# Gated DeltaNet layer: diagonal blocks stored apart in whole pieces, and VectorE's order beside the inversion written down

## The chip, the cores and the metric

The kernel runs on one core of a Trainium2 chip. The metric is the device time of one execution in microseconds, as the median of several runs. Engines are named by what they are: TensorE (PE) multiplies matrices, VectorE (DVE), ScalarE (ACT) and GpSimd (POOL) work on elements, SyncE (SP) only issues transfers. Each engine has its own queue of instructions, and ScalarE and POOL issue transfers from theirs too.

## What is computed

One layer of an encoder trunk: a sequence of 1024 tokens of width 1024, float32, with two mixers in parallel (grouped-query attention and a gated DeltaNet), and an expert-choice mixture behind them. The change lies in the DeltaNet. It has 8 heads of 64, works in chunks of 64 tokens in both directions, and needs for each chunk, head and direction the inverse of a unit triangular 64x64 matrix I + N. Beside it go the projections of the attention and the gates, and the modulation of the layer by a conditioning vector:

```
mod = silu(c) @ W_ada + b_ada -> (shift1, scale1, gate1, shift2, scale2, gate2)
h  = RMSNorm(x) * (1 + scale1) + shift1
one combined projection h @ W_in -> [attn q | attn k | attn v | dn q | dn k | dn v | dn z | dn beta(fwd,bwd) | dn decay(fwd,bwd) | branch gates]
A: GQA (8 q heads, 2 kv heads, dim 64), ...
B: gated DeltaNet (8 heads, dk=dv=64), ... forward and backward chunked scans with separate beta/decay parameters, summed, ...
merged = sigmoid(gA) * (A @ W_attn_up) + sigmoid(gB) * (B @ W_dn_up);  x += gate1 * (merged @ W_o)
```

## The kernel before

The part that matters runs from 100 to 410 us. First come the twelve projections of the DeltaNet (dn_group), bound by TensorE. Then eight tiles of 128 tokens (dn_tile, j = 0 to 7): for each tile and direction d VectorE makes masks (rr), TensorE sums them (L486), ScalarE takes an exponential (e, L488), VectorE multiplies (e, at, e, nn; L490 to L498). The tile nn holds two chunks of N for 8 heads; it is stored to n_d in device memory by two DMAs on SP's queue (L500). Beside tiles 0, 2 and 4 (QKV) a projection of the attention goes in (qkv_group).

A 64x64 matrix is inverted by its two diagonal 32x32 blocks and one product. dn_blocks reads the diagonal blocks back from n_d so that each of 128 partitions (16 chunks by 8 heads) holds the two blocks of one chunk and head (the tiles nb): four DMAs after tile 5, four after tile 7, issued by ScalarE, in pieces of 32 numbers, 128 bytes. dn_invert then works on VectorE alone: 31 steps q, in each a multiplication (L533) and a subtraction (L537) for either direction; it is a generator that gives way in 8 places (INV), so it has parts 0 to 7: steps 1 to 6, 7 to 10, 11 to 13, 14 to 16, 17 to 19, 20 to 22, 23 to 26, 27 to 31.

Between the parts stand eight "fills": projections of the attention (qkv_group 3 to 5) and gates (gate_group 0 to 4). Each is 48 matmuls (24 pairs, 8 depth blocks of 3 products: high part of the weights by high and low part of the activations, low part of the weights by the high part). proj_load loads 512 KB of weights on POOL's queue (wraw, L269), ScalarE casts the high part (wh, L272) and VectorE subtracts it (the low part wl, L273). wh and wl have two buffers each. proj_ahead loads the next group's weights early and notes them in self.ahead, which holds one entry:

```python
    def proj_ahead(self, col):
        self.ahead = col, self.proj_load(col)
    def proj(self, col, n=128):
        if self.ahead and self.ahead[0] == col:
            wh, wl = self.ahead[1]
            self.ahead = None
        else:
            wh, wl = self.proj_load(col, n)
```

The loop asks for the next group's weights, then runs a group, then a part of the inversion, then two steps of the modulation (mod(MODS[1])). A modulation step adds a row block of W_ada times the conditioning vector to macc (L903, L905); each eighth also closes a block: ScalarE casts the sum to a high part (L889), POOL subtracts for the low part (L890), TensorE adds over partitions (L892), SP loads the bias into y (L894), VectorE adds (L895), SP stores. These y tiles, and those that hold a fill's result until it is stored (L1121, L1163), share two buffers.

A scheduler orders the instructions of each engine by priorities and its own times, except inside a manual_schedule block, which keeps the program's order on the engines named: before, each of the 31 steps is one such block on VectorE, and the scheduler may place other work between them. After the inversion w_d is stored, and the scan follows; its first transposes are L606, and while it runs late_fill gives TensorE more projections (L1147).

Of the kernel before, what the change touches and what calls it, by code (L numbers as in the profile page):

```python
# [20 lines left out]
NT = 8  # L21
# [58 lines left out]
class K:  # L80
# [386 lines left out]
    def dn_tile(self, j):  # L467
# [13 lines left out]
        for d in range(2):  # L481
# [17 lines left out]
            for x in range(2):  # L499
                nc.sync.dma_start(self.n_d[d, 2 * j + x].rearrange("h s c -> s h c"),  # L500
                                  nn[64 * x:64 * x + 64].rearrange("p (h c) -> p h c", c=64))

    def dn_blocks(self, j0, j1):

        for d in range(2):
            src = self.n_d[d, 2 * j0:2 * j1].rearrange("n h (b s) c -> (n h) b s c", b=2)
            for b in range(2):
                self.nc.scalar.dma_start(self.nb[d][16 * j0:16 * j1, b], src[:, b, :, b * 32:b * 32 + 32])

    def dn_invert(self, pool, parts):  # L510
# [13 lines left out]
        for q in range(1, 32):  # L524
            sub = []
            with self.tc.manual_schedule(engines={mybir.EngineType.DVE}):
                for d, (nb, w, tmp) in enumerate(zip(nbs, ws, tmps)):
                    j = 32 - q if d == 0 else q - 1
                    rows = slice(0, j) if d == 0 else slice(j + 1, 32)
                    cols = slice(j, 32) if d == 0 else slice(0, j + 1)  # L530
                    shp = [128, 2, rows.stop - rows.start, cols.stop - cols.start]
                    t = tmp[:, :, rows, cols]
                    nc.vector.tensor_mul(t, nb[:, :, rows, j:j + 1].to_broadcast(shp),  # L533
                                         w[:, :, j:j + 1, cols].to_broadcast(shp))
                    sub.append((w[:, :, rows, cols], t))
                for t, u in sub:
                    nc.vector.tensor_sub(t, t, u)  # L537
            cost += q * (32 - q) + 60
            if cost >= total / parts:
                cost -= total / parts  # L540
                yield
# [31 lines left out]
    def scan_load(self, t):  # L573
# [6 lines left out]
        for d in range(2):  # L580
# [4 lines left out]
            nsrc = self.n_d[d, n].rearrange("h (b s) (e c) -> b s h e c", b=2, e=2)  # L585
# [3 lines left out]
            nc.sync.dma_start(nf[f], nsrc[d, :, :, 1 - d, :])  # L589
# [396 lines left out]
    def mixer(self):  # L986
        nc, i = self.nc, self.i
        with ExitStack() as stm:
# [10 lines left out]
            self.n_d = dnp.tile([2, 16, 8, 64, 64], F, name="n_d")  # L999
# [23 lines left out]
            def mod(n):  # L1023
                for _ in range(n):
                    next(mods, None)

            with ExitStack() as st2:
# [15 lines left out]
                for j in range(NT):  # L1043
                    if j in QKV:
                        self.qkv_group(QKV.index(j))
                    self.dn_tile(j)
                    if j == 5:
                        self.dn_blocks(0, 4)
                self.dn_blocks(4, NT)
            with ExitStack() as st2:  # L1050
                fills = [(self.qkv_group, C_Q, g) for g in range(3, 6)]
                fills += [(self.gate_group, C_G, g) for g in range(NGA)]
                iv = self.pool(st2, "invert", side="right")
                inv = self.dn_invert(iv, INV)
                for n, (f, c, g) in enumerate(fills):
                    if n + 1 < len(fills):
                        with self.tc.high_priority(offset=0):
                            self.proj_ahead(fills[n + 1][1] + fills[n + 1][2] * 128)
                    f(g)
                    next(inv, None)  # L1060
                    mod(MODS[1])
                for _ in inv:
                    pass
                mod(1000)
                self.lo = nc.vector
# [559 lines left out]
```

## Time and profile before

| | before |
|---|---|
| median of 3 runs | 1783.05 us (1782.53 to 1787.27) |
| profiled execution | 1782.9 us |
| its span in the profile | 1780.7 us |
| busy: TensorE, VectorE, ScalarE, POOL | 93%, 82%, 52%, 14% of the span |
| mean granted clock of TensorE | 0.965 of full speed |

The profile lists one execution: the span is what the engines' records cover, and 2.2 us of the execution lie around it. Busy time of one engine says nothing about what it waited for; that is read from the waits and the timelines, where each idle time is put down to the instruction or transfer whose end released the engine.

### The profile page before, as it was taken

The page shows a single profiled execution, that of the slowest core. Times are in us where ns is not written, and L with a number is a line of the kernel's source. Part 1 is how long each engine was busy: PE and PEld are TensorE (multiplying, and loading weights), DVE is VectorE, ACT ScalarE, POOL GpSimd, SP SyncE. Part 2 cuts the span into 40 slices and gives each one's busy share as a digit, 9 for nine tenths or more (in the row PEclk, how much of TensorE's full clock was granted, in tenths as well). Part 3 has the DMA queues.
Part 4 walks back from the last instruction along what each step waited for, and adds up shares of the span by engine and source line. Part 5 has one row for each costly group of instructions (what it writes and reads, how often), then busy time and mean ns, then how long its engine had stood idle before and what let it go on. Part 6 is the DMA issues. An engine that isn't in the chain of part 4 may idle for free. (4 is left out here: it accounts for less than half of the span.)

```text
span 1780.7 us, 28660 instructions
## 1 busy us (share of the span) xinstructions
PE 1663.8 (93%) x10363; PEld 1333.4 (75%) x10363; DVE 1453.2 (82%) x2523; ACT 924.4 (52%) x1372; POOL 256.7 (14%) x287
## 2 busy tenths in 40 slices
PE   6999998389999999999999999939999999999997
PEld 4777876377887778778887778827777777777776
DVE  6899895965777667679998366889999999999997
ACT  5654522113332422268884133327777777777775
POOL 0041512021111100021111212220000110010000
PEclk8999999699999999899999999969999999999999
DMA  9466389256667775431114454569999999999991
GB/s 272 124 178 178 108 214 212 71 174 166 192 188 180 206 224 134 137 124 34 34 35 160 159 204 155 191 238 309 387 387 383 370 384 385 382 373 379 387 335 24
DMA packets 283053, 390.81 MB, mean 219 GB/s; under 512 B 78299, under 2 KB 151695, under 8 KB 282655
## 3 DMA queue, kind: packets, MB, share of 16 engines
q1 hardware_dynamic: 247103, 328.15, 55.5%
q0 software_dynamic: 12960, 47.19, 9.7%
q10 hardware_dynamic: 22848, 13.63, 2.7%
q8 instruction: 82, 1.34, 0.3%
q14 instruction: 60, 0.49, 0.1%
HBM read 330.14 MB, written 58.77 MB: 218 GB/s over the span
## 5 line engine op out<-in xcount | busy, mean ns | idle before, releaser
L1514 DVE TENSOR_TENSOR ew<-er,ew 128x1024 fp32r<-128x1024 f32 x384 | 452.2, 1219 | 30.1 <-ACT ew L1513 30.1
L1513 ACT CAST ew<-er 128x1024 fp32r<-128x1024 f32 x384 | 391.1, 1049 | 138.2 <-PE pj L1567 103.0
L1567 PE MATMUL pj<-ew,xT 128*128 128x512 f32 x1536 | 368.0, 396 | 4.5 <-DVE ew L1514 4.5
L1567 PEld LDWEIGHTS pj<-ew,xT 128*128 128x128 f32 x1536 | 283.3, 188 | 76.4 <-DVE ew L1514 19.5
L1584 PE MATMUL tr<-ew,aT 128*128 128x512 f32 x768 | 191.3, 398 | 0.0
L1584 PEld LDWEIGHTS tr<-ew,aT 128*128 128x128 f32 x768 | 139.7, 188 | 30.5 <-DVE ew L1514 3.5
L279 PE MATMUL pj<-hTh,wl 128*128 128x512 f32 (+1 forms) x368 | 118.6, 401 | 26.4 <-DVE wl L273 26.4
L279 PE MATMUL pj<-hTh,wh 128*128 128x512 f32 (+1 forms) x368 | 118.5, 402 | 3.6 <-ACT hTh L252 1.8
L279 PE MATMUL pj<-hTl,wh 128*128 128x512 f32 (+1 forms) x368 | 118.6, 399 | 1.4 <-DVE hTl L255 1.4
L272 ACT CAST wh<-wraw 128x1024 fp32r<-128x1024 f32 (+1 forms) x45 | 46.7, 1037 | 137.3 <-PE pj L279 66.5
L279 PEld LDWEIGHTS pj<-hTh,wl 128*128 128x128 f32 (+1 forms) x368 | 69.3, 189 | 43.5 <-DVE wl L273 27.0
L1590 POOL DMA_INDIRECT out_dram<-xe,idxT x16 | 37.1, 2317 | 405.6 <-DVE tok L1488 351.1
L269 POOL DMA_DIRECT2D wraw<-in_w_in_dram x42 | 37.7, 898 | 369.4 <-DVE wl L273 278.7
L834 DVE TENSOR_REDUCE am<-pj 128x1 f32<-128x1024 f32 x64 | 77.8, 1217 | 12.4 <-PE pj L829 11.8
L1193 PE MATMUL pj<-hTh,uw 128*128 128x512 f32 x256 | 83.5, 404 | 1.0 <-DVE uth L1199 0.5
L279 PEld LDWEIGHTS pj<-hTh,wh 128*128 128x128 f32 (+1 forms) x368 | 68.6, 190 | 19.8 <-ACT hTh L252 1.9
L1147 PE MATMUL pj<-hTh,wh 128*128 128x512 f32 x240 | 82.7, 412 | 0.0
L1147 PE MATMUL pj<-hTh,wl 128*128 128x512 f32 x240 | 81.9, 410 | 0.0
L279 PEld LDWEIGHTS pj<-hTl,wh 128*128 128x128 f32 (+1 forms) x368 | 68.7, 188 | 17.6 <-DVE hTl L255 2.0
L1147 PE MATMUL pj<-hTl,wh 128*128 128x512 f32 x240 | 81.3, 409 | 0.0
L836 ACT ACTIVATE ap<-pj,am 128x1024 f32<-128x1024 f32 x64 | 71.9, 1123 | 13.9 <-DVE am L834 8.5
L829 PE MATMUL pj<-kT,qT 128*128 128x512 f32 x256 | 77.0, 412 | 1.5 <-ACT ap L836 1.5
(373 smaller groups left out, 3144.5 us busy)
## 6 DMA issues: line engine op xcount, KB each, us to landing
er<-in_w_gate_dram SPq DMA_DIRECT2D x128, 512.0 KB, 7.2
er<-in_w_up_dram SPq DMA_DIRECT2D x128, 512.0 KB
er<-in_w_down_dram SPq DMA_DIRECT2D x128, 512.0 KB, 10.0
wraw<-in_w_in_dram POOLq DMA_DIRECT2D x42, 512.0 KB, 5.8
mw<-in_w_ada_dram SPq DMA_DIRECT2D x64, 256.0 KB, 3.6
wt<-in_w_ada_dram SPq DMA_DIRECT2D x16, 512.0 KB, 8.6
gate_d<-y ACTq DMA_DIRECT2D x32, 256.0 KB, 3.3
kv<-kv_d SPq DMA_DIRECT2D x32, 256.0 KB, 3.6
```

The lines of the kernel that those rows point to most:

```text
L269: (queue or nc.gpsimd).dma_start(raw[:, :, :n], self.i["w_in"][0, :, col:col + n].rearrange("(k p) c -> p k c", p=128))
L272: nc.scalar.copy(wh[:, :, :n], raw[:, :, :n])
L279: self.nc.tensor.matmul(ps[q][:n], w[:, k, :n], x[k][:, q * 512:(q + 1) * 512], start=(k == 0 and w is wh and x is self.hTh), stop=(k == 7 ...
L829: nc.tensor.matmul(ps[:, kh], qT[:, i * 128:(i + 1) * 128], self.kT[a][:, s, kh * 512:(kh + 1) * 512], start=(s == 0), stop=(s == 1), skip ...
L834: nc.vector.reduce_max(m, ps, axis=AX.X, negate=True)
L836: nc.scalar.activation(p, ps, AF.Exp, bias=m, scale=1.0, accum_out=self.rv[:, h, half * 4 + i:half * 4 + i + 1])
L1147: nc.tensor.matmul(ps[q], a[:, k], x[k][:, q * 512:(q + 1) * 512], start=(k == 0 and a is wh and x is self.hTh), stop=(k == 7 and a is wl))
L1193: nc.tensor.matmul(ps, w[:, k], v[k][:, qs], start=(k == 0 and p == 0), stop=(k == 3 and p == 2))
L1513: nc.scalar.copy(hi, raw)
L1514: nc.vector.tensor_sub(lo, raw, hi.bitcast(F))
L1567: nc.tensor.matmul(pg[m], x[:, 2 * kp + k], wi[:, k], start=(kp == 0 and k == 0 and n == 0), stop=(kp == 3 and k == 1 and n == 2))
L1584: nc.tensor.matmul(py[q], x[:, k], wi[:, q], start=(k == 0 and n == 0), stop=(k == 7 and n == 2))
```

## The change

It does four things. N is stored in parts: the two diagonal blocks of each chunk go to a new tensor nb_d, laid out as the inversion reads it, by four DMAs on SP's queue; the one off-diagonal quarter that the scan needs goes to a smaller n_d by two DMAs on POOL's queue. dn_blocks reads whole pieces of 8 KB per partition, on SP's queue, after tiles 2, 4, 6 and 7. The manual order on VectorE reaches around the whole loop of fills, inversion parts and modulation, so all of VectorE's work there keeps the program's order. And the weights of the first fill are asked for after tile 4.

```diff
             for x in range(2):
-                nc.sync.dma_start(self.n_d[d, 2 * j + x].rearrange("h s c -> s h c"),
-                                  nn[64 * x:64 * x + 64].rearrange("p (h c) -> p h c", c=64))
+                n = 2 * j + x
+                rows = lambda b, e: nn[64 * x + 32 * b:64 * x + 32 * b + 32].rearrange(
+                    "p (h c) -> p h c", c=64)[:, :, 32 * e:32 * e + 32]
+                for b in range(2):
+                    nc.sync.dma_start(self.nb_d[d, 8 * n:8 * n + 8, b].rearrange("h s c -> s h c"), rows(b, b))
+                nc.gpsimd.dma_start(self.n_d[d, n].rearrange("h s c -> s h c"), rows(d, 1 - d))
...
         for d in range(2):
-            src = self.n_d[d, 2 * j0:2 * j1].rearrange("n h (b s) c -> (n h) b s c", b=2)
-            for b in range(2):
-                self.nc.scalar.dma_start(self.nb[d][16 * j0:16 * j1, b], src[:, b, :, b * 32:b * 32 + 32])
+            self.nc.sync.dma_start(self.nb[d][16 * j0:16 * j1].rearrange("p b s c -> p (b s c)"),
+                                   self.nb_d[d, 16 * j0:16 * j1].rearrange("n b s c -> n (b s c)"))
...
         for q in range(1, 32):
             sub = []
-            with self.tc.manual_schedule(engines={mybir.EngineType.DVE}):
...
-            nc.sync.dma_start(nf[f], nsrc[d, :, :, 1 - d, :])
+            nc.sync.dma_start(nf[f], self.n_d[d, n].rearrange("h s c -> s h c"))
...
-                    if j == 5:
-                        self.dn_blocks(0, 4)
-                self.dn_blocks(4, NT)
+                    if j == QKV[-1]:
+                        self.proj_ahead(C_Q + len(QKV) * 128)
+                    if j in (2, 4, 6):
+                        self.dn_blocks(j - 2, j)
+                self.dn_blocks(6, NT)
...
-                for n, (f, c, g) in enumerate(fills):
...
+                with self.tc.manual_schedule(engines={mybir.EngineType.DVE}):
+                    for n, (f, c, g) in enumerate(fills):
+                        if n + 1 < len(fills):
+                            with self.tc.high_priority(offset=0):
+                                self.proj_ahead(fills[n + 1][1] + fills[n + 1][2] * 128)
+                        f(g)
+                        next(inv, None)
+                        mod(MODS[1])
+                    for _ in inv:
+                        pass
+                    mod(1000)
```

On VectorE, where the inversion begins, the order before has two low parts ahead of the memsets and one more between the first two multiplications (wtmp, wb and nb are the inversion's tiles; 128x2x31 is step 1):

```order
L273 TENSOR_TENSOR wl_3099<-wraw_3096,wh_3098 128x1024
L273 TENSOR_TENSOR wl_3105<-wraw_3102,wh_3104 128x1024
L520 MEMSET wb0_2838 128x32 x2
L520 MEMSET wb1_2843 128x32 x2
L533 TENSOR_TENSOR wtmp0_2842<-nb0_707,wb0_2838 128x2x31
L905 TENSOR_SCALAR macc_712<-mw2_711,cs_182 128x512
L273 TENSOR_TENSOR wl_3191<-wraw_3188,wh_3190 128x1024
L533 TENSOR_TENSOR wtmp1_2847<-nb1_708,wb1_2843 128x2x31
```

Afterwards, at the end of part 0 and of part 1 (steps 6 and 10), VectorE's order reads:

```order
L539 TENSOR_TENSOR wb1_2916<-wb1_2916,wtmp1_2920 128x2x26x6
L906 TENSOR_SCALAR macc_713<-mw0_710,cs_183 128x512
L904 SCALAR_TENSOR_TENSOR macc_713<-mw1_711,cs_183,macc_713 128x512
L273 TENSOR_TENSOR wl_2952<-wraw_2949,wh_2951 128x1024
L273 TENSOR_TENSOR wl_2958<-wraw_2955,wh_2957 128x1024
L535 TENSOR_TENSOR wtmp0_2915<-nb0_708,wb0_2911 128x2x25x7
...
L539 TENSOR_TENSOR wb1_2916<-wb1_2916,wtmp1_2920 128x2x22x10
L896 TENSOR_TENSOR y_3039<-y_3039,tr_3032 1x512
L904 SCALAR_TENSOR_TENSOR macc_713<-mw2_712,cs_183,macc_713 128x512
L904 SCALAR_TENSOR_TENSOR macc_713<-mw0_710,cs_183,macc_713 128x512
L273 TENSOR_TENSOR wl_3050<-wraw_3047,wh_3049 128x1024
L273 TENSOR_TENSOR wl_3056<-wraw_3053,wh_3055 128x1024
```

No low part stands ahead of the inversion any more; two stand behind each part, and the modulation's addition (L896 of the change) has a fixed place behind part 1.

On TensorE, behind the last of the tiles' products (L478), the order of the change begins with a matmul that reads one of these low parts, wl_2958, and the modulation's two matmuls (L893) stand four matmuls into the next group:

```order
L478 MATMUL dn_2759<-kq3_720 64x64 x4
L279 MATMUL pj_2961<-hTh0_405,wl_2958 128x512 x2
L279 MATMUL pj_2961<-hTh1_446,wh_2957 128x512 x2
...
L279 MATMUL pj_2961<-hTh7_675,wl_2958 128x512 x2
L279 MATMUL pj_3059<-hTh0_405,wh_3055 128x512 x2
L279 MATMUL pj_3059<-hTl0_406,wh_3055 128x512 x2
L893 MATMUL tr_3032<-y_3033,one_65 1x512
L893 MATMUL tr_3032<-y_3034,one_65 1x512
L279 MATMUL pj_3059<-hTh0_405,wl_3056 128x512 x2
```

Before, the same place has the rest of a group whose weights were there already, and the next group behind it:

```order
L478 MATMUL dn_2694<-kq3_719 64x64 x4
L279 MATMUL pj_2906<-hTl5_610,wh_2902 128x512
L279 MATMUL pj_2906<-hTh5_609,wl_2903 128x512 x2
...
L279 MATMUL pj_2906<-hTh7_674,wl_2903 128x512 x2
L279 MATMUL pj_3016<-hTh0_404,wh_3012 128x512 x2
```

So TensorE's work behind the tiles now starts with a low part that VectorE makes behind part 0 of the inversion; before, it had its low parts.

## Rows read from the trace of the kernel before

**Rows 1.** The page, part 1: busy us, share of the span, instructions.
```profile
PE 1663.8 (93%) x10363; PEld 1333.4 (75%) x10363; DVE 1453.2 (82%) x2523; ACT 924.4 (52%) x1372; POOL 256.7 (14%) x287
```

**Rows 2.** Waits of TensorE, 220 to 410 us: total us, times, longest us.
```profile
PE pj L279 <- DVE wl L273: 26.4, 1, 26.4
PE tr L892 <- POOL y L890: 5.0, 3, 4.0
```

**Rows 3.** Windows: from:to, us, busy us of PE, PEld, DVE, ACT, POOL, clock, DMA, GB/s.
```profile
320.00:345.00 25.00, 1.78 (x4) 1.49 (x5) 25.00 (x46) 0.60 (x1) 0.89 (x1) 0.50 0.05 21
...
400.00:500.00 100.00, 98.36 (x981) 79.33 (x980) 68.76 (x165) 32.84 (x69) 13.82 (x20) 1.00 0.68 177
```

**Rows 4.** VectorE's timeline: start us, us of one, work, count, idle before and releaser.
```profile
284.41 1.23 DVE L273 TENSOR_TENSOR wl<-wraw,wh 128x1024 fp32r<-128x1024 f32 x1 [2.85 <-ACT wh L272]
...
286.76 0.75 DVE L498 TENSOR_TENSOR nn<-dn,e 128x256 f32<-128x256 f32 x2
...
290.35 0.76 DVE L498 TENSOR_TENSOR nn<-dn,e 128x256 f32<-128x256 f32 x2
...
292.53 0.76 DVE L498 TENSOR_TENSOR nn<-dn,e 128x256 f32<-128x256 f32 x2
...
309.41 0.28 DVE L533 TENSOR_TENSOR wtmp<-nb,wb 128x62 f32<-128x62 f32 x1 [7.35 <-DMA nb<-n_d]
...
313.08 0.28 DVE L533 TENSOR_TENSOR wtmp<-nb,wb 128x62 f32<-128x62 f32 x1 [0.60 <-DVE wl L273]
...
319.65 0.94 DVE L533 TENSOR_TENSOR wtmp<-nb,wb 128x350 f32<-128x350 f32 x2
...
327.37 0.67 DVE L895 TENSOR_TENSOR y<-y,tr 1x512 f32<-1x512 f32 x1
...
341.96 1.21 DVE L273 TENSOR_TENSOR wl<-wraw,wh 128x1024 fp32r<-128x1024 f32 x1
```

**Rows 5.** TensorE's timeline around the gap and at the end of the fills.
```profile
289.09 0.62 PE L279 MATMUL pj<-hTh,wl 128*128 128x512 f32 x2
...
309.51 0.61 PE L279 MATMUL pj<-hTh,wl 128*128 128x512 f32 x2
...
343.22 1.22 PE L279 MATMUL pj<-hTh,wl 128*128 128x512 f32 x2 [26.45 <-DVE wl L273]
...
347.30 0.62 PE L279 MATMUL pj<-hTl,wh 128*128 128x512 f32 x2
...
395.76 0.62 PE L1147 MATMUL pj<-hTh,wh 128*128 128x512 f32 x2
...
408.90 0.69 PE L606 MATMUL tr<-Sc 32*32 32x32 f32 x16
```

**Rows 6.** ScalarE's timeline, its DMA queue (ACTq) included.
```profile
294.91 13.87 ACTq L508 DMA_DIRECT2D nb<-n_d  x4
...
321.49 0.60 ACT L1162 ACTIVATE y<-pj 128x512 f32<-128x512 f32 x1 [2.06 <-DMA gate_d<-y]
```

**Rows 7.** Lines L500 and L589: landing us, issue duration in ns (min/median/max).
```profile
DMA to landing us min/median/max: 3.2/4.3/6.3
...
L589 SPq DMA_DIRECT2D Sc<-n_d x32: 303/450/1217, 403.1 to 722.3; - x32
```

**Rows 8.** Timelines of POOL, SyncE (SPq) and VectorE: the modulation's sum.
```profile
309.53 1.29 POOL L890 TENSOR_TENSOR y<-macc,y 128x512 fp32r<-128x512 f32 x1 [7.72 <-ACT y L889]
...
370.36 5.53 POOL L890 TENSOR_TENSOR y<-macc,y 128x512 fp32r<-128x512 f32 x1 [1.05 <-ACT y L889]
...
375.91 0.24 SPq L894 DMA_DIRECT2D y<-in_b_ada_dram  x1
...
377.38 0.68 DVE L895 TENSOR_TENSOR y<-y,tr 1x512 f32<-1x512 f32 x1 [2.62 <-PE tr L892]
```

**Rows 9.** The page, parts 5 and 6: weight loads, and one 256 KB load.
```profile
L269 POOL DMA_DIRECT2D wraw<-in_w_in_dram x42 | 37.7, 898 | 369.4 <-DVE wl L273 278.7
...
kv<-kv_d SPq DMA_DIRECT2D x32, 256.0 KB, 3.6
```

More of the change, by code (lines that the diff above doesn't have):

```diff
@@ L525, in dn_invert @@
             sub = []
-            with self.tc.manual_schedule(engines={mybir.EngineType.DVE}):
[L527 to L537, printed above, removed]
+            for d, (nb, w, tmp) in enumerate(zip(nbs, ws, tmps)):
+                j = 32 - q if d == 0 else q - 1
+                rows = slice(0, j) if d == 0 else slice(j + 1, 32)
+                cols = slice(j, 32) if d == 0 else slice(0, j + 1)
+                shp = [128, 2, rows.stop - rows.start, cols.stop - cols.start]
+                t = tmp[:, :, rows, cols]
+                nc.vector.tensor_mul(t, nb[:, :, rows, j:j + 1].to_broadcast(shp),
+                                     w[:, :, j:j + 1, cols].to_broadcast(shp))
+                sub.append((w[:, :, rows, cols], t))
+            for t, u in sub:
+                nc.vector.tensor_sub(t, t, u)
             cost += q * (32 - q) + 60
@@ L584, in scan_load @@
             src = self.w_d[d].rearrange("(n h) (b s c) -> n b s h c", h=8, b=2, s=32)
-            nsrc = self.n_d[d, n].rearrange("h (b s) (e c) -> b s h e c", b=2, e=2)
             for b in range(2):
@@ L998, in mixer @@
             self.a_d = dnp.tile([2, NT, 128, 512], F, name="a_d")
-            self.n_d = dnp.tile([2, 16, 8, 64, 64], F, name="n_d")
+            self.n_d = dnp.tile([2, 16, 8, 32, 32], F, name="n_d")
+            self.nb_d = dnp.tile([2, 128, 2, 32, 32], F, name="nb_d")
             self.w_d = dnp.tile([2, 128, 2048], F, name="w_d")
@@ L1054, in mixer @@
                 inv = self.dn_invert(iv, INV)
-                for n, (f, c, g) in enumerate(fills):
[L1056 to L1064, printed above, removed]
+                with self.tc.manual_schedule(engines={mybir.EngineType.DVE}):
[9 more added lines that the diff above has]
+                    mod(1000)
                 self.lo = nc.vector
```

## The prediction

> **What bounds the kernel now.** The page first: TensorE is busy 93% of the span and VectorE 82% [rows 1], so a change pays where TensorE stands still. The waits of TensorE from 220 to 410 us have one large entry, 26.4 us once, for the low part of a projection's weights (wl, L273); the next takes 5.0 us in three waits, one of them 4.0 [rows 2]. The table by windows places it: from 320 to 345 us TensorE works 1.78 us of 25 and VectorE all 25 [rows 3]. VectorE's timeline says why: VectorE is inside the inversion, and the low part that TensorE needs stands behind 16 of its 31 steps, at 341.96 [rows 4]; TensorE goes on at 343.22 [rows 5]. So in this stage neither engine is the bound for long: from the tiles' end at 289 to the last matmul of the fills at 395.8 they work in turn. What the change is worth is when the fills end (the first L1147 matmul stands at 395.76 now), because the scan's first matmul follows it on TensorE (408.90 [rows 5]), and TensorE works 98.4 of the 100 us from 400 [rows 3]: a later start isn't made good.
>
> **The end of the tile phase.** The last product nn ends at 292.53 + 0.67 = 293.2 [rows 4]. Of the work in front of it, three low parts go (six stand between the tiles now, three afterwards): 3 x 1.14 = 3.4 us, since the work behind each starts 1.13 to 1.15 later. The 2.85 us that VectorE waits for a weight's high part at 284.41 [rows 4] goes with them. That makes 286.95, and I take 287.0: what the low parts cover now of the tiles' own turns between TensorE, ScalarE and VectorE comes to light, and ScalarE's part of these turns no longer stands behind block loads; I set the one against the other. Bounds: only the second of these, some 3 us as long as the one wait of rows 4, 284; the 32 new stores on POOL's queue and 64 more on SP's holding back a buffer of nn, 293.
>
> **The diagonal blocks.** Now ScalarE issues the last four block loads for 13.87 us and VectorE waits 7.35 us for them, so the first multiplication is at 309.41, the second at 313.08 behind a low part [rows 4, 6]. Afterwards the last tile's four stores are issued by SP; the row nearest in shape, the scan's load of 32x8x32, takes 0.45 us to issue [rows 7], so the last starts 1.2 after the first. Their landing is bounded by the present stores of N, 3.2 to 6.3 us, median 4.3 [rows 7]; being half as large, I take 3.9. The read of whole pieces then lands like another 256 KB load, 3.6 [rows 9]. With 0.1 to start: 287.0 + 0.1 + 1.2 + 3.9 + 3.6 = 295.8, 13.6 us earlier than the first and 17.3 earlier than the second now. POOL has only its two memsets of wb to do meanwhile. The Trainium skill ("DMA: Bandwidth & Descriptors", Why small descriptors are slow) speaks for this part: pieces under 512 bytes are slow against memory. The trace agrees, with 13.87 us of issue for pieces of 128 bytes. It prices the read alone; the sum goes by the rows.
>
> **The order on VectorE.** Here the gain is lost. VectorE's instructions now stand in the order of the program: part 0 of the inversion, two sums of the modulation (macc), a low part, another low part; part 1; an addition (L896 of the change); two sums; two low parts; part 2; and so on. Two facts of the code make this dear. First, the attribute that holds weights loaded ahead has one place, and the next load overwrites it before the group that wanted it has asked. So the first of each two low parts is thrown away (1.14 us of VectorE, and a 512 KB load), and only the second is used; both before and after (42 weight loads [rows 9], of which six are thrown away; the new early one is thrown away too and makes 43). Second, that used one always lands in the pair of buffers that the group in work reads, so its high part is cast when TensorE is through with that group, and VectorE stands there. The scheduler of before puts other work in front of such a wait; a fixed order can't.
>
> So TensorE has seven groups of 24 pairs of matmuls left behind the tiles: two pairs of the first run between them, and 22 pairs wait for the first group's low part, which stands behind part 0. That is 166 pairs; before, 152 were left at 289. A pair takes (309.51 - 289.09) / 45 = 0.454 us [rows 5]. The parts last, from the present rows: part 0 6.6 (313.08 to 319.65), part 1 7.7 (to 327.37), parts 2 and 3 together 14.6 with an addition of 0.6 ahead of them (327.37 to 341.96) [rows 4]. Later parts lie beside TensorE's groups as these two do. A sum is taken as 0.65, by its 512 elements to the addition's.
>
> From the first multiplication at 295.8, in us:
> part 0 and two sums to 303.4, the two low parts to 305.7. TensorE begins the first group there, 22 pairs for 10.0, and 2.0 more for a spell at the half clock: after the present gap of 26.45 us the next 4.08 us (343.22 to 347.30) do five pairs, which take 2.27 otherwise, and the clock granted there is 0.50 of full speed, the lower of its two levels, 1.2 GHz [rows 3, 5]; 2.0 is a little over the 1.8 lost. It ends at 317.8. VectorE ends part 1 at 313.4 and stands.
> What it waits for is the addition, and that chain is long: group's end, 0.85 for the cast of the next weights on ScalarE, the copy of the result (0.6), its store until it lands (2.06 that ScalarE waits for it at 321.49 [rows 6]) since the cast of macc needs the same buffer, that cast 0.6, POOL's subtraction 1.3 [rows 8], a matmul, the load of the bias 1.5 (375.91 to 377.38 [rows 8]), the addition 0.65. VectorE is free at 325.7; two sums and two low parts make 329.3. TensorE stood 11.5 us.
> Second group: 22 pairs and a slow spell, 12.2, ends 341.5. VectorE has part 2 and the sums done at 337.4, and the used low part ends 2.0 behind the group's end, at 343.5.
> Third to fifth group alike, 22 pairs 10.0 and a handover of 2.0 to 2.1: 365.7 is the low part of the fifth, whose last matmul is at 377.8.
> Then the second chain of an addition, 7.8, a sum or two and two low parts: 389.2. The sixth group has its 22 pairs, the last one's weights really are ahead: 44 pairs, 20.0, and a slow spell of 2.0. The fills end at **411.1**, 15.3 later than 395.8.
>
> The scan's first loads follow through the same chain as before (modulation, SP's queue), so this goes on to the end one for one. The profiled execution took 1782.9 us (span 1780.7 and 2.2 around it), 0.15 below the median of the runs, 1783.05. Forecast: 1782.9 + 15.3 = **1798** us.
>
> A rule against the change on POOL's side: the Trainium skill ("SBUF — State Buffer", SBUF: two separate sides) says that a DMA issued from GpSimd starves for its descriptors while VectorE holds the port that both share. Here POOL's subtraction takes 5.53 us beside the inversion against 1.29 alone [rows 8], which agrees with such a port, but a weight load is issued by POOL in 898 ns on average [rows 9], with VectorE busy 82% of the span, and issues show no such wait. By the rule the new stores on POOL would be late; that is the third rival.
>
> **Rivals.**
> *The additions don't hold VectorE (the other side, faster).* If both find their operands early, as at 327.37 now, where the addition has no wait [rows 4], each chain of 11.5 us of standing TensorE shrinks to a handover of 2.0, and the slow spell behind it goes: 2 x (9.4 + 2.0) = 22.8 less, the fills end near 389, 7 earlier than now: 1776. Were the used weights also in the free pair of buffers, TensorE would run on from 305.7 for 166 pairs, 75.3, to 381 or 383: 1769. For it: the 26.45 us are there to be had. Against it: the order puts each addition behind a group whose result must be stored first, and at 377.38 VectorE waits 2.62 for it even now [rows 8]. It decides by whether the cast of macc has a buffer before the group's result is stored.
> *The gap only moves (no change).* One of the two additions finds its operands, the other doesn't: 411.1 - 11.4 = 399.7, 1787, inside what can be told apart. For it: the two stand behind groups of different kinds (a projection of q, k, v and a gate). Against it: both kinds are stored by ScalarE from the same two buffers.
> *The stores of N hold the tiles up (slower still).* VectorE's products nn of one direction of a tile follow each other by 3.6 us (286.76 to 290.35 [rows 4]) into two buffers in turn, so a buffer's six stores have some 6.5 us (two such steps less the products' own 0.7) to be issued and to land. Median landing, 4.3, behind four or five issues of 0.45 is 6.1 to 6.6. If POOL's issues are late as well, each of eight tiles gives up about one us: 8 more, 1806. POOL's 5.53 for 1.29 would be 4 more per addition if it came while VectorE works; here VectorE stands, so that is left out.
>
> **How the numbers follow.** Forecast 0.60, its own range 1788 to 1808: end of tiles 284 to 293 (-3, +6), landing (-1, +2), slow spells none or one per group (-6, +4), bounds that will not all fall on one side. Stores hold up 0.12, the gap only moves 0.15, faster 0.13. What this kernel can tell from no change is 0.3%, 5.3 us. From the cases: slower 0.70 (the forecast less a little of its low end, and the late stores), same 0.17, faster 0.13. Two in ten may lie outside: the faster case (1776 and 1769) below, half of the late stores above: 1778 to 1809.
>
> **What the profile would show.** Right: the first multiplication near 296; the 26.45 gap replaced by one of some 19 behind the tiles and two of some 11; VectorE waiting for TensorE's L893 before L896 twice, and for ScalarE's cast of wh before every second low part; 43 weight loads; the fills ending near 411; nothing else moved but by that. Wrong: VectorE without waits between the parts, or the addition's operands early (then the same or faster); VectorE waiting for a store before nn, or the last nn after 293 (then slower by the third rival); a scan that starts no later although the fills end later, which would mean that its start hangs on something else.

## The result and the profile after

The change is slower: 1805.35 us (median of 4 runs, 1801.68 to 1808.36) against 1784.09 us before (also the median of 4), ratio 1.0116, 95% interval 1.009 to 1.0142. The forecast was 1798 in a range of 1778 to 1809. The profiled execution has a span of 1802.0 us, 21.3 more than before.

The page of the change: busy times (columns as in [rows 1]) and the weight loads, of which there is one more than before [rows 9]:

```profile
PE 1672.3 (93%) x10363; PEld 1336.2 (74%) x10363; DVE 1458.8 (81%) x2524; ACT 926.6 (51%) x1373; POOL 270.9 (15%) x320
...
L269 POOL DMA_DIRECT2D wraw<-in_w_in_dram x43 | 38.6, 898 | 346.6 <-DVE wl L273 271.0
```

The shares hardly move; the waits tell. Those of TensorE, then of VectorE, from 210 to 430 us after the change (total us, times, longest us):

```profile
PE pj L279 <- DVE wl L273: 33.7, 4, 23.9
PE tr L893 <- ACT y L890: 8.3, 3, 5.3
PE dn L478 <- DVE nn L498: 5.1, 1, 5.1
PE pj L279 <- ACT wh L272: 4.7, 4, 2.7
```

```profile
DVE y L896 <- DMA y<-in_b_ada_dram: 25.8, 3, 12.0
DVE wl L273 <- ACT wh L272: 9.5, 5, 5.8
```

The one gap of 26.45 us [rows 2, 5] has become three (23.93, 5.26 and 4.29; the fourth of the view, 0.2, lies between the tiles), and VectorE, which had no wait for an addition at 327.37 [rows 4], now stands 12.05 and 10.53 us at the two additions of the stage and 3.2 at a third behind it, each time until the bias has landed. VectorE's timeline shows where:

```profile
292.19 0.76 DVE L498 TENSOR_TENSOR nn<-dn,e 128x256 f32<-128x256 f32 x2 [0.59 <-DMA nb_d<-nn]
...
300.30 0.26 DVE L535 TENSOR_TENSOR wtmp<-nb,wb 128x62 f32<-128x62 f32 x1 [2.10 <-DMA nb<-nb_d]
302.06 0.26 DVE L535 TENSOR_TENSOR wtmp<-nb,wb 128x62 f32<-128x62 f32 x1 [1.50 <-DMA nb<-nb_d]
...
309.74 2.35 DVE L273 TENSOR_TENSOR wl<-wraw,wh 128x1024 fp32r<-128x1024 f32 x2
...
331.87 0.67 DVE L896 TENSOR_TENSOR y<-y,tr 1x512 f32<-1x512 f32 x1 [12.05 <-DMA y<-in_b_ada_dram]
332.47 1.52 DVE L904 SCALAR_TENSOR_TENSOR macc<-mw,cs,macc 128x512 f32<-128x512 f32 x2
333.91 2.35 DVE L273 TENSOR_TENSOR wl<-wraw,wh 128x1024 fp32r<-128x1024 f32 x2
...
389.00 0.67 DVE L896 TENSOR_TENSOR y<-y,tr 1x512 f32<-1x512 f32 x1 [10.53 <-DMA y<-in_b_ada_dram]
```

The inversion does begin earlier, its second multiplication at 302.06 against 313.08 [rows 4]. Behind the sixth step come two sums and two low parts, and behind the tenth VectorE stands 12.05 us; only then can the two low parts at 333.91 be made. TensorE's timeline shows the other side of each wait:

```profile
312.15 1.22 PE L279 MATMUL pj<-hTh,wl 128*128 128x512 f32 x2 [23.93 <-DVE wl L273]
...
328.88 0.59 PE L893 MATMUL tr<-y,one 128*1 128x512 f32 x1 [1.98 <-ACT y L890]
330.47 0.59 PE L893 MATMUL tr<-y,one 128*1 128x512 f32 x1 [1.01 <-POOL y L891]
...
336.31 1.22 PE L279 MATMUL pj<-hTh,wl 128*128 128x512 f32 x2 [5.26 <-DVE wl L273]
...
392.32 2.36 PE L279 MATMUL pj<-hTh,wl 128*128 128x512 f32 x4 [4.29 <-DVE wl L273]
...
414.34 0.62 PE L1152 MATMUL pj<-hTh,wh 128*128 128x512 f32 x2
```

TensorE begins the first fill at 312.15, 1.3 us after the second low part of 309.74 begins, waits again around the modulation's matmuls (L893), and the fills end at 414.34, 18.6 us later than before (395.76 [rows 5]). The scan's first transposes stand at 434.09, 25.2 later; the attention begins 23.9 later and the expert layers 21.2.

### The profile page after: what moved, and what is told of

Read it like the earlier page. It is cut to its first block, busy times and chain, and to the rows that moved or that the text cites. A ratio compares the mean times of both kernels' runs of the same rounds, so it can differ in the third digit from the quotient of the medians.

```text
span 1802.0 us, 28781 instructions
## 1 busy us (share of the span) xinstructions
PE 1672.3 (93%) x10363; PEld 1336.2 (74%) x10363; DVE 1458.8 (81%) x2524; ACT 926.6 (51%) x1373; POOL 270.9 (15%) x320
## 5 line engine op out<-in xcount | busy, mean ns | idle before, releaser
L279 PEld LDWEIGHTS pj<-hTh,wh 128*128 128x128 f32 (+1 forms) x368 | 68.3, 190 | 23.9 <-ACT wh L272 6.6
L1152 PE MATMUL pj<-hTl,wh 128*128 128x512 f32 x240 | 85.0, 419 | 0.0
L835 DVE TENSOR_REDUCE am<-pj 128x1 f32<-128x1024 f32 x64 | 77.9, 1218 | 8.5 <-PE pj L830 7.9
```

The lines of the kernel that those rows point to most:

```text
L279: self.nc.tensor.matmul(ps[q][:n], w[:, k, :n], x[k][:, q * 512:(q + 1) * 512], start=(k == 0 and w is wh and x is self.hTh), stop=(k == 7 ...
L835: nc.vector.reduce_max(m, ps, axis=AX.X, negate=True)
L1152: nc.tensor.matmul(ps[q], a[:, k], x[k][:, q * 512:(q + 1) * 512], start=(k == 0 and a is wh and x is self.hTh), stop=(k == 7 and a is wl))
```

## The experiments

Eleven of them, each on one chip with the kernel before. One table serves all. "Tiles" is the time from the last reduction of the DeltaNet's projections (L335) to the end of the last nn; it runs from the beginning of that reduction, which executions reach up to 4 us apart (217.8 to 221.9). "Start" is the inversion's second multiplication, "end" the first matmul of late_fill, "stage" the time between, "scan" its first transposes; these are read from the timelines of one profiled execution each. The ratio to the kernel before is from timed runs.

| kernel | tiles | start | end | stage | scan | span | ratio (95%) |
|---|---|---|---|---|---|---|---|
| before | 71.7 | 313.1 | 395.8 | 82.7 | 408.9 | 1780.7 | 1 |
| the change | 71.7 | 302.1 | 414.3 | 112.3 | 434.1 | 1802.0 | 1.0116 (1.009 to 1.0142) |
| 1 the change again | 73.4 | 300.4 | 413.4 | 113.0 | 431.9 | 1792.8 | 1.0093 (1.0054 to 1.0133) |
| 2 order alone | 66.1 | 295.5 | 407.8 | 112.3 | 427.4 | 1785.8 | 1.0053 (1.003 to 1.0077) |
| 3 storage alone | 77.9 | 319.1 | 389.4 | 70.3 | 407.5 | 1771.8 | 0.9981 (0.9958 to 1.0004) |
| 4 stores on SyncE | 78.7 | 310.3 | 422.8 | 112.5 | 441.2 | 1802.6 | 1.0101 (1.0065 to 1.0137) |
| 5 no early load | 68.4 | 297.9 | 410.1 | 112.2 | 429.7 | 1791.4 | 1.0077 (1.0048 to 1.0106) |
| 6 loads kept | 71.0 | 297.2 | 373.2 | 76.0 | 395.3 | 1779.0 | 1.0058 (1.0033 to 1.0082) |
| 7 late addition | 70.8 | 298.1 | 401.5 | 103.4 | 420.7 | 1776.2 | 0.9984 (0.9964 to 1.0004) |
| 8 late, on SyncE | 77.7 | 309.5 | 411.8 | 102.3 | 432.0 | 1785.6 | 1.0042 (1.0013 to 1.0071) |
| 9 late, no early load | 68.0 | 297.5 | 399.9 | 102.4 | 420.1 | 1773.6 | 0.9966 (0.9938 to 0.9994) |
| 10 late, nothing ahead | 66.2 | 295.0 | 382.8 | 87.8 | 402.0 | 1777.5 | 0.9939 (0.9917 to 0.996) |
| 11 late, in pairs | 71.9 | 300.2 | 393.3 | 93.0 | 412.5 | 1767.8 | 0.9918 (0.9886 to 0.995) |

### Order, storage, and the change again (kernels 1 to 3)

Kernel 1 is the change, unaltered.

> The change itself once more, on the chip of the other kernels, since one execution's length scatters. Theory A (the written order sets the stage): from the second multiplication of the inversion to the end of the fills 112.3 us again, as in the change and in the kernel with the order alone; 1.0 to 1.4% slower than before. If the difference were an accident of one execution, the stage would have another length.

Stage 113.0, ratio 1.0093, a little under the 1.0 to 1.4% expected. The slowdown is no accident of one execution.

Kernel 2 has the written order on the storage of before (manual_schedule around the loop, none in the steps, no early load):

```diff
-            with self.tc.manual_schedule(engines={mybir.EngineType.DVE}):
...
+                with self.tc.manual_schedule(engines={mybir.EngineType.DVE}):
+                    for n, (f, c, g) in enumerate(fills):
```

> Before with VectorE's written order alone: storage, stores and block loads as before, no early weights. Theory A (the order costs: VectorE stands at the two additions and at the used low parts): the tiles end at 288 to 293, the first multiplication 16.2 us behind them as before (so 305 to 309), and the fills end some 112 us behind it, as they do after the change (414.3 - 302.1): 417 to 421, which is 1804 to 1812 us. Theory B (the new stores cost: they delay weights and tiles, and the order is harmless): no slower than before, 1783 or less.

Slower, 1.0053, and the stage has the length of the change to the tenth, 112.3, without any of the new storage: the order sets it. That part of theory A held, theory B fell. The time, 1791.9 us (median), lies 12 below the 1804 to 1812 expected, since the first multiplication, at 292.4, comes over 12 us before the 305 to 309 expected: the tiles end at 284.1, and the blocks take 8.3 us behind them in place of 16.2. ScalarE issues the last four block loads in 5.81 us here (before 13.87 [rows 6]):

```profile
285.65 5.81 ACTq L508 DMA_DIRECT2D nb<-n_d  x4
```

They are the same loads, in pieces of 128 bytes, so the 13.87 us in which the prediction saw the slowness of small pieces aren't the price of the pieces alone; what else they hold is not shown. Counted from the last reduction of the projections, the start is at 77.5 us here and at 77.7 in kernel 5, which has the new storage and no early load either. Under the written order no gain of the new storage shows at the start.

Kernel 3 is the change without the order and the early load.

```diff
-                with self.tc.manual_schedule(engines={mybir.EngineType.DVE}):
-                    for n, (f, c, g) in enumerate(fills):
...
-                    if j == QKV[-1]:
-                        self.proj_ahead(C_Q + len(QKV) * 128)
```

> The change without the written order and without the early weights: only the new storage and the new block loads. Here the scheduler's order puts all low parts up to the sixth fill ahead of the inversion and the seventh's behind part 6. Theory A: the inversion then can't begin before TensorE has read the fifth fill, some 330, though its blocks are there at 300; TensorE stands about 40 us for the seventh fill, and the fills end near 410: 1795 to 1800, slower than before by another order, not by the stores. Theory B: as slow as the change, 1805, with the tiles ending at 293 or later. The profile tells them apart by what the first multiplication waits for: a low part (A), or the block loads (B).

The time was missed: 0.9981, no difference that can be told, in place of a slowdown. The expected place of the wait was right, its price not. VectorE waits for casts ahead of the inversion, though the blocks' loads are over (its timeline):

```profile
312.49 1.23 DVE L273 TENSOR_TENSOR wl<-wraw,wh 128x1024 fp32r<-128x1024 f32 x1 [7.30 <-ACT wh L272]
314.83 1.23 DVE L273 TENSOR_TENSOR wl<-wraw,wh 128x1024 fp32r<-128x1024 f32 x1 [1.11 <-ACT wh L272]
...
316.98 0.26 DVE L536 TENSOR_TENSOR wtmp<-nb,wb 128x62 f32<-128x62 f32 x1
```

The first multiplication came at 317 and not behind 330, and TensorE's largest wait was 14.45 us, not 40; the fills ended 6.4 us earlier than before. The new storage left to the scheduler is no loss. (The tiles are long here, 77.9, with eight low parts between them.)

That largest wait is not for a low part but for POOL's subtraction of the modulation's sum, which takes 14.64 us here and 1.29 alone [rows 8] (POOL's, VectorE's and TensorE's timelines of kernel 3):

```profile
348.12 14.64 POOL L892 TENSOR_TENSOR y<-macc,y 128x512 fp32r<-128x512 f32 x1 [28.87 <-DMA gate_d<-y]
...
364.34 0.68 DVE L897 TENSOR_TENSOR y<-y,tr 1x512 f32<-1x512 f32 x1 [2.70 <-PE tr L894]
...
362.82 0.59 PE L894 MATMUL tr<-y,one 128*1 128x512 f32 x1 [14.45 <-POOL y L892]
```

VectorE works through the inversion without a pause until 361.64 (364.34 less the 2.70 of waiting), and the subtraction ends 1.12 us later, at 362.76. It comes through only when VectorE stands; kernel 7 shows the same.

### What lengthens the tiles (kernels 4 and 5)

Kernel 4 issues the off-diagonal stores from SyncE:

```diff
-                nc.gpsimd.dma_start(self.n_d[d, n].rearrange("h s c -> s h c"), rows(d, 1 - d))
+                nc.sync.dma_start(self.n_d[d, n].rearrange("h s c -> s h c"), rows(d, 1 - d))
```

> The change with the off-diagonal stores on SyncE's queue in place of POOL's. Theory C (the stores on POOL hold up the weight loads behind them, so ScalarE's cast and exponential come late and the tiles end at 292.9 in place of 287): the wait of 3.9 us for the exponential goes and the tiles take 3 to 5 us less. Theory D (the early weight load alone does it: a third load in two buffers, cast ahead of an exponential in ScalarE's queue): the wait stays, the tiles take as long. The 112.3 us behind the first multiplications stay in both. Time 1795 to 1805.

Kernel 5 leaves out the early load:

```diff
-                    if j == QKV[-1]:
-                        self.proj_ahead(C_Q + len(QKV) * 128)
```

> The change without the early weight load behind tile 4; stores on POOL stay. Theory D: the wait of 3.9 us for the exponential goes and the tiles end 3 to 6 us earlier, as they do with the order alone. Theory C: they take as long as in the change. The 112.3 us behind stay. Time 1795 to 1805.

Neither theory foresaw kernel 4's tiles: they take 78.7 us, longer than in the change. The six stores then stand in one queue, and VectorE waits 4.0 us for buffers of nn, in kernel 4 (waits of VectorE, 215 to 300 us):

```profile
DVE nn L498 <- DMA n_d<-nn: 2.1, 2, 1.4
DVE nn L498 <- DMA nb_d<-nn: 1.9, 1, 1.9
```

So kernel 4 brings a loss of its own and can't decide by itself. Theory C falls by kernel 5, whose stores are still on POOL, and by the timelines: POOL issues the two weight loads whose casts come before the exponential at 249.53 and 251.66, no later than the kernel before, whose queue holds no stores, issues its two, at 250.09 and 251.96 (POOL's timeline of the change, then of the kernel before):

```profile
249.53 0.89 POOL L269 DMA_DIRECT2D wraw<-in_w_in_dram  x1 [0.84 <-issue]
```

```profile
250.09 0.89 POOL L269 DMA_DIRECT2D wraw<-in_w_in_dram  x1 [22.69 <-DVE e L490]
```

Theory D held: without the early load the tiles take 68.4, and VectorE's longest wait for an exponential is 1.3 us (waits of VectorE in kernel 5, 215 to 300 us):

```profile
DVE e L490 <- ACT e L488: 3.0, 4, 1.3
```

In the change a cast that kernel 5 doesn't have there, the one at 259.90, stands on ScalarE just ahead of an exponential (ScalarE's timeline, then VectorE's row that waits for it):

```profile
256.61 1.05 ACT L272 CAST wh<-wraw 128x1024 fp32r<-128x1024 f32 x1 [2.68 <-DMA wraw<-in_w_in_dram]
259.90 1.05 ACT L272 CAST wh<-wraw 128x1024 fp32r<-128x1024 f32 x1 [2.25 <-DMA wraw<-in_w_in_dram]
260.85 0.59 ACT L488 ACTIVATE e<-tr 128x512 f32<-128x512 f32 x1
```

```profile
261.47 0.69 DVE L490 TENSOR_TENSOR e<-e,masks 128x512 f32<-128x512 f32 x1 [3.91 <-ACT e L488]
```

In ScalarE's queue the exponential stood behind a cast that waited for weights. The early load costs 2.4 to 5.4 us: 70.8, 71.7 and 73.4 in kernel 7, the change and kernel 1, against 68.4 and 68.0 in kernels 5 and 9. What the storage adds to the tiles can't be told from the scatter of single executions: kernel 5 takes 2.3 us more than kernel 2, but kernel 10, which has the storage too and one low part of 1.14 us fewer between the tiles, takes 66.2 against kernel 2's 66.1.

### The additions (kernels 7 to 9)

Kernel 7 leaves casts, subtraction and matmuls of the modulation where they are, and puts VectorE's addition one fill later:

```diff
-            nc.vector.tensor_add(mb, mb, ps[0:1])
-            nc.sync.dma_start(self.mod_d[row:row + 1, qs], mb)
+            self.owed.append((n + self.lag, mb, ps, row, qs))
+        while self.owed and self.owed[0][0] <= n:
+            _, mb, ps, row, qs = self.owed.pop(0)
+            nc.vector.tensor_add(mb, mb, ps[0:1])
+            nc.sync.dma_start(self.mod_d[row:row + 1, qs], mb)
```

> The change with the modulation's addition (and the store behind it) one fill later in the program; casts, subtraction and matmuls stay. Theory A: VectorE's waits of 12.0 and 10.5 us at the additions go, TensorE's two stretches without work there (11.3 and 9.4 us) shrink to handovers of 2, with the slow spells behind them: 16 to 20 us less, 1785 to 1790. Theory B: no change, 1805.

The loss is gone: 1778.2 us (median), 0.9984, better than the 1785 to 1790 expected. In the stage, though, only 8.9 us are saved (112.3 to 103.4) where 16 to 20 were expected. POOL's subtraction, which lies between the cast and the matmul, is the main reason; its rows in the change, then in kernel 7, there with VectorE's additions behind it:

```profile
329.16 1.26 POOL L891 TENSOR_TENSOR y<-macc,y 128x512 fp32r<-128x512 f32 x1 [15.88 <-DMA qkv_d<-y]
386.32 1.26 POOL L891 TENSOR_TENSOR y<-macc,y 128x512 fp32r<-128x512 f32 x1 [13.26 <-DMA gate_d<-y]
```

```profile
325.02 3.64 POOL L892 TENSOR_TENSOR y<-macc,y 128x512 fp32r<-128x512 f32 x1 [3.11 <-ACT y L891]
376.81 4.98 POOL L892 TENSOR_TENSOR y<-macc,y 128x512 fp32r<-128x512 f32 x1 [2.15 <-PE pj L279]
...
330.15 0.68 DVE L900 TENSOR_TENSOR y<-y,tr 1x512 f32<-1x512 f32 x1 [2.62 <-DMA y<-in_b_ada_dram]
...
383.41 0.67 DVE L900 TENSOR_TENSOR y<-y,tr 1x512 f32<-1x512 f32 x1 [2.74 <-PE tr L894]
```

While VectorE stands, it takes 1.26 us; beside the inversion 3.64 and 4.98. VectorE stands from 327.53 and from 380.67 (the additions' starts less their waits), and the subtractions end 1.13 and 1.12 us behind that. TensorE waits for them 7.3 us in the stage; with the 8.9 saved that makes 16.2. So an addition placed later still makes VectorE stand, 2.62 and 2.74 us, as the chain behind it gets through only then.

Kernel 8 has the edits of 4 and 7, kernel 9 those of 5 and 7.

> The change with the addition one fill later and the off-diagonal stores on SyncE's queue: what both together bring. Theory A: the stage behind the first multiplications 103 us as with the late addition alone; with theory C the tiles 3 to 5 us shorter as well: 1770 to 1776, faster than before. With theory D as the late addition alone, within 0.3% of before.

> The change with the addition one fill later and without the early weight load. Theory A and D together: tiles as without the early load, the stage behind the first multiplications 103 us as with the late addition alone: 3 us less than with the late addition alone, 1774 to 1778; the two low parts per part of the inversion, one of them thrown away, stay, and VectorE still waits 15 to 23 us in all for casts of high parts.

Kernel 8, 1.0042, is in neither of its ranges: it is slower than 7 by its tiles, 77.7, which lengthen as in kernel 4; its stage, 102.3, is that of the late addition. Kernel 9 came out as expected, 0.9966, faster than before, VectorE waiting 16.3 us for casts (290 to 420 us), 7.8 of them in the stage.

### The weights loaded ahead (kernels 6, 10 and 11)

Kernel 6 keeps what is loaded ahead:

```diff
-        self.ahead = col, self.proj_load(col)
+        self.ahead[col] = self.proj_load(col)
...
-        if self.ahead and self.ahead[0] == col:
-            wh, wl = self.ahead[1]
-            self.ahead = None
+        if col in self.ahead:
+            wh, wl = self.ahead.pop(col)
```

> The change with weights loaded ahead kept until they are asked for (a dictionary for the one place): no load is thrown away, the used low part lies in the free pair of buffers. Theory A: the first fill's low part is made between the tiles, the gap of 24 us behind them shrinks to the second fill's, the handovers go, and the two additions find their operands since a fill's result is stored long before; the fills end at 375 to 380 and the time is 1765 to 1772. Theory B: the stores are unchanged, only 7 x 1.14 us of VectorE go: 1795 to 1800.

In the stage most came as expected: 76.0 us, the fills' end at 373.2, a little before the 375 to 380 expected, though one gap of 21.8 us for a low part stays and one addition still waits 5.6. The time did not: 1.0058, slower than before. The fills end 22.5 us earlier and the attention starts later, at 751.6 against 747.3. The scan starts at 395.3, not at the fills' end, and in TensorE's order 84 matmuls of late_fill stand ahead of it (48 in the change and before). From 540 to 560 us none of late_fill's matmuls runs (39 do in the change); TensorE stands there, 5.5 us of it at once for VectorE, and gets the lower clock (windows of kernel 6; columns as in [rows 3]):

```profile
520.00:540.00 20.00, 18.59 (x183) 15.03 (x181) 13.49 (x31) 6.15 (x12) 3.68 (x5) 0.99 0.72 177
540.00:560.00 20.00, 13.49 (x135) 11.94 (x136) 13.60 (x37) 4.88 (x11) 3.03 (x4) 0.50 0.63 152
560.00:580.00 20.00, 19.22 (x143) 16.45 (x142) 9.23 (x20) 5.61 (x12) 0.00 (x0) 0.57 0.50 146
```

From the fills' end to the attention the mean granted clock is 0.92 in kernel 6 and 0.99 in the kernel before; over the whole execution it is 0.949 to 0.965 in its ten runs against 0.961 to 0.971 before. That the matmuls spent ahead of the scan are what is missing at 540 was not tested by a kernel.

Kernel 10 is kernel 9 without loading ahead (the "run before" of its expectation is kernel 9); kernel 11 is kernel 9 with each second fill's weights loaded ahead. First the edit of 10, then that of 11:

```diff
-                        if n + 1 < len(fills):
-                            with self.tc.high_priority(offset=0):
-                                self.proj_ahead(fills[n + 1][1] + fills[n + 1][2] * 128)
```

```diff
-                        if n + 1 < len(fills):
+                        if n + 1 < len(fills) and n % 2 == 0:
                             with self.tc.high_priority(offset=0):
```

> The kernel of the run before without loading ahead at all, so each fill loads only its own weights, and these now fall into the pair of buffers that the fill before doesn't use. Theory A (the thrown-away load pushes the used weights onto the busy pair): VectorE's waits for casts go although nothing is loaded ahead any more, each of the seven handovers of some 2 us goes, and the stage shrinks from 103 to about 91 us: 1762 to 1770, faster than before. If the waits are weights that come late from memory, less loading ahead makes them longer: 1780 or more.

> As the kernel without loading ahead, but each second fill's weights are loaded ahead and used: the first fill's low part stands between the tiles, so TensorE's gap of 23.6 us behind the tiles is filled by 22 pairs, and another of some 18 follows until part 1 is through. Theory A: 90 to 93 us from the second multiplication to the end of the fills, the gap cut in two but hardly shorter: 1762 to 1772.

Kernel 10 loads less ahead and waits less: TensorE has one wait for a low part left (21.6 us, behind the tiles) and no handover, VectorE waits for no cast in the stage (7.8 us in kernel 9), stage 87.8 against 102.4. So the waits for casts came from the pair of buffers, not from late weights. Part of the gain is POOL's subtraction, which takes 1.28 us again as VectorE stands at the additions meanwhile: TensorE waits 0.3 us for it in the stage, 4.3 in kernel 9. The ratio is 0.9939 (1772.1, 2 above the range); its interval overlaps kernel 9's. Kernel 11: stage 93.0 as forecast, ratio 0.9918 (1769.55). The forecast of its gap was wrong: it isn't cut in two, TensorE waits once, 31.0 us, behind a fill run earlier. Both are faster than the kernel before and than the change; their intervals don't tell the two apart.

## Why the prediction came out as it did

**What bounds the stage** held. TensorE and VectorE work in turn, and the low part behind a stretch of the inversion is what TensorE waits for, 23.93 us now (counted from TensorE's last product of the tiles; from the last nn it is 19.3, with 18.7 forecast).

**The end of the tiles** is the term that was wrong: 287.0 forecast, 292.86 measured, at its bound of 293. Three low parts did go, but nothing in the sum stood for the early load, whose cast in ScalarE's queue ahead of an exponential made VectorE wait 3.91 us. Kernel 2, which has neither the early load nor the stores, takes 66.1 us; the forecast's 287.0 means 65.5 from the same point of before (293.2 - 71.7 = 221.5). The working, with "I set the one against the other", was right for the order alone and wrong for the early load, which it priced by its low part only. The bound of 293 was reached for another reason than the one it names, stores that hold back nn.

**The diagonal blocks**: 8.8 us from the last nn to the first multiplication were forecast, 7.4 measured. Not foreseen was that the two directions' loads end apart, so the second multiplication comes 1.76 later; the stage started 6.3 us late.

**The order** was right in mechanism and nearly in size: 115.3 us forecast from start to end, 112.3 measured, and 112.2 to 113.0 in every kernel with this order, this loading ahead and this place of the additions. Shifted by the late start, the first fill at 305.7 becomes 312.0 (measured 312.15), the first addition's end 325.7 becomes 332.0 (332.5), the second group's low part 329.3 becomes 335.6 (TensorE goes on with it at 336.31). The second addition, expected to end at 391.9 so shifted, ends at 389.6: the four groups between took some 2 us less. VectorE waited for the bias's load, the last link of the chain, where the prediction expected the wait to be put down to the matmul ahead of it.

**The sum**: fills' end 411.1 forecast, 414.3 measured; + 15.3 against + 18.6. The difference is made of four misses that partly cancel: the tiles + 5.9, the blocks - 1.4, the second direction + 1.8, the stage - 3.0. Two small slips lie in the working: three issues of 0.45 are 1.35 and not 1.2, and part 0 with two sums ends at 303.7 and not 303.4.

The scan followed, later still, since a third sum's matmuls stand ahead of it on TensorE, which waits 5.27 us for ScalarE's cast at 424.54 (0.69 before). That the shift goes on to the end one for one is not shown, and that the time came so near has luck in it. In the profiled execution of the change the fills end 18.6 us later and the span is 21.3 longer, but a spell at the lower clock in the scan (below, some 12 us) is part of that; in kernel 1 the fills end 17.7 us later, the attention begins 14.3 later and the span is 12.1 longer. The intervals of both ratios, 1.0116 and 1.0093, hold a shift of 18 us; only kernel 1's holds the forecast's 15.3. In kernel 6 a gain of 22.5 us became a loss: there 84 matmuls of late_fill stand ahead of the scan, in the change the same 48 as before.

**The rivals.** That the additions don't hold VectorE was priced at 22.8 us; moved one fill later, they gave 8.9, since POOL's subtraction doesn't get through beside the inversion. The prediction left this out, rightly for the change, where VectorE stands and the subtraction takes 1.26 us. That stores hold back nn showed as 0.59 us in the change and as 4.0 with all six on SyncE, where 8 had been priced; the steps of 3.6 us by which that rival has the products nn follow each other aren't the rule, the next is 2.2 (290.35 to 292.53 [rows 4]). The Trainium skill ("SBUF — State Buffer", SBUF: two separate sides) says two things on POOL's side. Its lock between VectorE and GpSimd, under which the second to come is fully blocked, agrees with subtractions of 3.64, 4.98 and 14.64 us that end 1.1 us after VectorE falls still. That DMAs issued from GpSimd starve it states for VectorE's operations in a two-port mode, a condition that the prediction left out; no run here shows such starving. The stores on POOL's queue (line L505 of the change; ns min/median/max):

```profile
L505 POOL DMA_DIRECT2D n_d<-nn x32: 585/585/602, 228.4 to 293.8; - x32
```

**What stays open.** From the fills' end to the attention kernels 7 to 9 and 11 take 342 to 344 us, the kernel before 351.5, the change 356.9 and 348.1. Part of it is TensorE's clock in the scan, which differs between two executions of the same kernel (below). The late addition alone doesn't explain it: kernel 10 has it too and takes 351.8, in a profiled execution that is the longest of its runs. So the ratios of 7, 9 and 11 are better than their fills' ends, 5.7 and 4.1 us later and 2.5 earlier than before, and this difference isn't explained.

## What to carry to other kernels

A written order takes the scheduler's freedom to step around a wait, so before writing one, list for each instruction in it what it waits for, and put a long chain's last link (here an addition behind a cast, a subtraction on another engine and a small load) a whole stage later. Then look again at the chain's other links, which may take longer beside an engine that now works on. A load ahead into a ring of two buffers that is thrown away was worse than none in this stage (102.4 us against 87.8): it turns the ring, so the load that is used falls into the buffers still in use. And a stage that ends earlier isn't worth its time by itself; kernel 6 suggests that the work that filled the next stage must not be used up by it.

## What the runs showed of the hardware

A POOL subtraction of 128x512 doesn't get through beside VectorE's inversion. Begun while VectorE works through it without a pause, it took 3.64 and 4.98 us (kernel 7), 5.53 (before [rows 8]) and 14.64 (kernel 3), and each time it ended 1.12 to 1.13 us after VectorE fell still; alone it takes 1.26 to 1.29. It isn't slowed in proportion: how long it takes is how long VectorE goes on. The other way round, a product of VectorE that takes 0.69 us took 1.65 in kernel 11 (at 285.82) while such a subtraction, begun at 285.66, ran.

TensorE gets the lower clock also while it never stands. In the scan of the change (windows; columns as in [rows 3]):

```profile
600.00:620.00 20.00, 19.08 (x222) 15.57 (x223) 11.96 (x29) 7.86 (x16) 2.69 (x5) 1.00 0.79 212
620.00:640.00 20.00, 19.94 (x206) 16.11 (x207) 10.96 (x23) 5.33 (x12) 1.60 (x2) 0.79 0.64 174
640.00:660.00 20.00, 20.00 (x147) 16.51 (x144) 9.85 (x13) 4.86 (x10) 2.50 (x2) 0.61 0.81 273
660.00:680.00 20.00, 20.00 (x181) 15.85 (x179) 13.89 (x42) 5.06 (x10) 0.89 (x1) 1.00 0.37 94
```

From 640 to 655 the granted clock is 0.50, the lower level of 1.2 GHz, with TensorE busy all the time:

```profile
640.00:650.00 10.00, 10.00 (x76) 8.10 (x72) 6.21 (x9) 3.28 (x7) 0.88 (x1) 0.50 1.03 375
650.00:655.00 5.00, 5.00 (x30) 4.36 (x29) 0.00 (x0) 1.58 (x3) 0.00 (x0) 0.50 0.77 249
```

It had just worked mostly through the scan's small products, 64x64 and 32x32; as kernel 1 does the same without a slow spell, what made the clock fall is not shown. The same kernel in another execution (kernel 1) has a clock of 1.00 in all of this stretch:

```profile
640.00:660.00 20.00, 20.00 (x189) 16.05 (x189) 13.96 (x34) 6.62 (x13) 2.44 (x2) 1.00 0.96 306
```

In the same 20 us it issues 189 matmul records against 147. By the windows' clocks the spell costs an estimated (1 - 0.79) x 20 + (1 - 0.61) x 20 = 12 us, so a single execution can't settle a difference of 0.5% here; the stage's own length, 112.2 to 113.0 in five kernels, can.
